# Chained gated MLP: the sums of the weight blocks as GpSimd adds, the chain's copies ahead of GeLU, the first blocks' splits behind the last softmax

## The chip, the cores and the metric

The kernel runs on one core of one Trainium2 chip. The metric is the device time of one execution in microseconds (us). Engines by the names of the profile: PE is TensorE (matmuls), PEld its weight loads, DVE is VectorE, ACT is ScalarE, POOL is GpSimd, SP issues most of the transfers. POOL can also issue transfers; a transfer issued there may add to what lies at its destination ("adding transfer" below).

## The reference, cut to what matters

Two layers; each has a token mixer, a cross-attention and a gated MLP. The change touches the gated MLP and the end of the attention ahead of it.

```python
def conv_ffn(x, norm, w_up, dw_w, dw_b, w_down):
    h = rms_norm(x, norm) @ w_up
    g = causal_dwconv(h[..., :D_FF], dw_w, dw_b)
    u = h[..., D_FF:]
    return (jax.nn.gelu(g) * u) @ w_down

def trunk(x, mem, ...):
    for layer in range(DEPTH):
        ...
        x = x + cross_attn(x, mem, ...)
        x = x + conv_ffn(x, f_norm[layer], f_w_up[layer], f_dw_w[layer], f_dw_b[layer], f_w_down[layer])
    ...
```

The sequence has 512 positions, D_MODEL is 1024, the hidden width D_FF is 3072, and everything is float32.

## The kernel before, in words

**Precision.** A float32 operand is split into a high part (a copy to fp32r by ACT, "high") and a low part (what is left, a subtraction by DVE, "low"). A product is three matmuls: high by high (L186), high by low (L187, L188).

**A unit of the MLP.** The hidden width is cut into 24 chunks of 128 columns per layer, and a unit c computes one chunk of the gate and of the up branch. Two of the 24 are computed plainly ahead (the opening); units 2 to 23 use a scheme of seven products in place of eight, in which sums of blocks of the weights meet sums of blocks of the activations. The blocks of the weights of a chunk are a11, a12, a22 and four sums, s1 to s4. A unit's products, in PE's order, are s1, s2, a12, s3, then (units with c of 4 and more) 24 matmuls of the down projection, then a11 of the next unit, s4, a22. They are chained through PSUM: a product's bank is copied on by ACT (L946, L960, L927), and the next product that accumulates in that bank waits for the copy.

**The sums of the weights.** Class Blocks holds the tiles of one chunk. `load` fetches one 512 KB tile `raw`, whose first half is `r` and whose second is `z`; `load_second` fetches a12 and a22 (tiles `wa`, 256 KB each). The sums are formed in place: once a block has been split by `high` (L814) and `low` (L821), `low` issues the next sum. After a11, z is added to r (L824). After s3, a22 is added to z and to r (L827, two adds). After s2, a12 is added to r (L829). Each of the four is an adding transfer that POOL issues, 256 KB from SBUF to SBUF. There are 22 chunks in each of two layers, so 176 of them; the attention (whose blocks are made with `ring`) uses the same class for 6 pairs, 24 transfers more.

**What sets the order.** Inside a unit the engines run what the code issues in that order: ACT, DVE and POOL are in order, and a waiting instruction holds up what stands behind it. `gating` is a generator that carries the elementwise work of unit c (gate convolution L894 and L897, GeLU L899, product L913, splits L916 and L918) into unit c+1; each `next(left)` in `unit` issues one step of it. The down projection's two banks are first loaded with X by ACT (`down.bank`, L854) and are copied home later (L859).

**The end of the attention.** `prepare` splits blocks of the first MLP chunk inside the attention. `scores(3)`, `transpose(3)`, `back(...)` are the last head's scores, its transposes and the output projections; `score.last` is the last instruction of the softmax so far issued, and `tc.issue_after` keeps what it encloses behind that instruction in program order.

Of the kernel before, what the change touches and what calls it, by code (L numbers as in the profile page):

```python
# [13 lines left out]
ALU = mybir.AluOpType  # L14
# [47 lines left out]
def trunk(ctx: ExitStack, tc: tile.TileContext, I: dict, out: list):  # L62
    nc = tc.nc
    V, A, G, PE = nc.vector, nc.scalar, nc.gpsimd, nc.tensor
# [30 lines left out]
    def tmp_f(n=T):  # L95
        return tmp.tile([P, n], F32, tag="tmp", name=nm("tmp"))

    def main_ps():
        return psum.tile([P, T], F32, tag="mm", name=nm("mm"))
# [70 lines left out]
    def add(out, a, b):  # L170
        V.tensor_tensor(out, a, b, op=ALU.add)  # L171
        return out
# [6 lines left out]
    def low(src, hi, lo=None):  # L179
        lo = act_r() if lo is None else lo  # L180
        V.tensor_tensor(lo, src, hi.bitcast(F32), op=ALU.subtract)  # L181
        return hi, lo
# [54 lines left out]
    class Scaled:  # L237
# [39 lines left out]
        def low(self, c):  # L277
            self.x[c] = low(*self.x[c])
# [191 lines left out]
    def attention(layer, norm, mem, nxt, six, up):  # L470
# [51 lines left out]
        def scores(h):  # L522
            for half in range(2):
                for _ in score(h, half):
                    pass
# [8 lines left out]
        def turned(h):  # L534
            hs = [high(pt) for pt in ps[h]]
            ps[h] = [low(*x) for x in zip(ps[h], hs)]
# [9 lines left out]
        def mixed(h):  # L546
            for d, out in enumerate(mix(h)):
                o[2 * h + d] = split(out)
# [40 lines left out]
        def unit(i, before):  # L589
# [59 lines left out]
            if i == 2:  # L649
                end(3, "a11")  # L650
            q[2 * h] = low(g, hi)
            p = m("a22", six.T4)
            transpose(i)
# [45 lines left out]
        def prepare(*names):  # L699
            for name in names:  # L700
                up.high(name)
                up.low(name)

        back(0, range(4))
        mixed(2)
        prepare("a11", "a22")
        scores(3)
        back(0, range(4, 6))
        back(4, range(6))
# [69 lines left out]
    class Blocks:  # L779
# [39 lines left out]
        def low(self, name):  # L819
            hi, lo = self.w[name]  # L820
            V.tensor_tensor(lo, self.block(name), hi.bitcast(F32), op=ALU.subtract)  # L821

            if name == "a11":
                G.dma_start(self.r, self.z, accum_op=ALU.add)  # L824
            elif name == "s3":
                for block in (self.r, self.z) if self.ring else (self.z, self.r):
                    G.dma_start(block, self.a22, accum_op=ALU.add)  # L827
            elif name == "s2":
                G.dma_start(self.r, self.a12, accum_op=ALU.add)  # L829

    def pairs_of(layer):
        return {c: Blocks(I["wpair"][layer * (CF - PLAIN) + c - PLAIN]) for c in range(PLAIN, CF)}
# [1 line left out]
    def ffn(layer, norm, nxt, seven, pairs):  # L834
# [37 lines left out]
        def high(c, name):  # L872
            if c in pairs and (c, name) not in done:
                pairs[c].high(name)

        def low(c, name):
            if c in pairs and (c, name) not in done:
                pairs[c].low(name)
                done.add((c, name))

        def both(c, name):
            high(c, name)
            low(c, name)

        def times_r(out, ps, at):
            V.tensor_tensor(out[:, at], ps, norm.r[:, at], op=ALU.mult)
# [15 lines left out]
        def gating(c, g, f, u, F, H):  # L902
            add(g[:, right_half], H, u[:, :M])
            V.tensor_tensor(g[:, right_half], g[:, right_half], norm.r[:, right_half], op=ALU.mult)
            conv = gate_conv(c, g)
            y = next(conv)
            yield
            times_r(f, F, left_half)
            next(conv)
            yield  # L910
            next(conv)
            yield
            V.scalar_tensor_tensor(y, f, -1.0, y, op0=ALU.mult, op1=ALU.mult)  # L913
            yield
            ys[c] = act_r(), act_r()
            A.activation(ys[c][0], y, AF.Copy)  # L916
            yield
            V.tensor_tensor(ys[c][1], y, ys[c][0].bitcast(F32), op=ALU.subtract)  # L918

        def m(c, ps, block, j, first=True):  # L920
            seven.product(ps, pairs[c].w[block], j, first)

        def ahead(c):

            G, F = main_ps()[:, :M], main_ps()[:, :M]
            m(c, G, "a11", seven.B11)
            A.activation(F, G, AF.Copy)  # L927
            return G, F

        def unit(c):  # L930

            nonlocal left, chains
            G, F = chains
            down, seeded = downs.get(c), c > GC
            H = main_ps()[:, :M]
            m(c, H, "s1", seven.T1)
            high(c + 1, "s3")
            next(left, None)
            low(c + 1, "s3")
            if c == first:  # L940
                both(c + 2, "a11")

            m(c, F, "s2", seven.T2, False)
            next(left, None)
            u, f, g = tmp_f(), tmp_f(), tmp_f()
            A.activation(u[:, :M], F, AF.Copy)  # L946
            next(left, None)
            high(c + 1, "a22")

            m(c, G, "a12", seven.B21, False)  # L950
            next(left, None)
            if down:
                d = [down.bank(i, seeded) for i in range(2)]
            next(left, None)
            low(c + 1, "a22")
            times_r(g, G, left_half)
            high(c, "s4")

            m(c, F, "s3", seven.T3, False)
            A.activation(u[:, M:], F, AF.Copy)  # L960
            low(c, "s4")
            add(f[:, right_half], H, u[:, M:])
            V.tensor_tensor(f[:, right_half], f[:, right_half], norm.r[:, right_half], op=ALU.mult)
            both(c + 2, "a11")
            high(c + 1, "a12")
            low(c + 1, "a12")
            if down:
                for ks in (range(GC - 1), (GC - 1,)):
                    for i in range(2):
                        down.products(i, d[i], seeded, ks)  # L970
            if c + 3 in pairs:
                pairs[c + 3].load()
            if c + 2 in pairs and c > first:
                pairs[c + 2].load_second()
            if c >= GC - 1 and c + 1 in downs:
                downs[c + 1].w.high()
                downs[c + 1].w.low()
            if c + 2 in downs and c + 2 <= CF:
                downs[c + 2].load()
            high(c + 1, "s1")  # L980
            low(c + 1, "s1")
            high(c + 1, "s2")
            low(c + 1, "s2")
            if down:
                down.home(0, d[0], seeded)

            if c + 1 in pairs:
                chains = ahead(c + 1)
            if down:
                down.home(1, d[1], seeded)  # L990

            m(c, H, "s4", seven.B22, False)
            m(c, F, "a22", seven.T4, False)
            left = gating(c, g, f, u, F, H)
            next(left)
# [81 lines left out]
        left, chains = None, None  # L1077
# [7 lines left out]
        with tc.manual_schedule(engines=ORDERED):  # L1085
            opening()
            for c in range(PLAIN, CF):
                unit(c)
            for _ in left:
                pass  # L1090
# [711 lines left out]
    six = mixer(n0, n1)  # L1802
    pairs = pairs_of(0)
    mem, parked = ffn(0, n2, n3, attention(0, n1, mem, n2, six, pairs[PLAIN]), pairs)
    six = conformer(n3, n4, mem, parked)
    pairs = pairs_of(1)
    ffn(1, n5, None, attention(1, n4, mem, n5, six, pairs[PLAIN]), pairs)


# [76 lines left out]
```

## Time and profile before

| what | us |
|---|---|
| median of 3 runs | 1436.37 (1435.02 to 1438.07) |
| the profiled execution's own time | 1440.97 |
| its span in the trace | 1439.2 |
| layer 0: attention, MLP | about 255 to 346, 346 to 740 |
| layer 1: attention, MLP | about 935 to 1036, 1040 to 1395 |

A row of the timeline reads: start, length (both us), engine, line of the kernel, operation, output and input tiles, their shape, and in brackets the idle time of the engine ahead of it with what ended it. Rows of one engine can overlap by some hundredths, since an instruction's fill and drain are counted. A row of the windows reads: the stretch and its length, then busy us and instructions of PE, PEld, DVE, ACT and POOL, then the granted clock of TensorE (1.00 is full), the busy share of the DMA engines, and GB/s.

### The profile page before, as it was taken

How to read it: one execution, taken by the hardware profiler on the slowest of the kernel's cores; microseconds unless marked ns; L12 is line 12 of the kernel's file. 1: busy time of each engine (PE TensorE's matmuls, PEld its weight loads, DVE VectorE, ACT ScalarE, POOL GpSimd, SP SyncE). 2: the span in 40 equal slices, each digit the busy share in tenths (PEclk: the TensorE clock that was granted, in tenths of full speed). 3: DMA queues.
4: the chain of work that ended last, by engine and by line, in shares of the span. 5: the costliest groups of instructions: out<-in, count | busy, mean ns of one | idle time of the engine just before them, and what ended most of it. 6: DMA issues, size and time to landing. Idle time of an engine off the chain costs nothing.

```text
span 1439.2 us, 22840 instructions
## 1 busy us (share of the span) xinstructions
PE 1421.0 (99%) x8650; PEld 1263.3 (88%) x8650; DVE 1079.1 (75%) x1796; ACT 910.2 (63%) x1592; POOL 317.4 (22%) x333
## 2 busy tenths in 40 slices
PE   9999999999999999999999999999998999999998
PEld 8888888988999999999888777899888999999997
DVE  6987776778876666666789997877787666676665
ACT  7668755667556666666655557667654666666664
POOL 0012310100122222222009991011002222222211
PEclk9999999999999999999999999999999999999999
DMA  8522242544487777777432364345438777777751
GB/s 302 194 88 89 88 132 69 118 108 146 115 197 170 173 175 166 170 176 155 133 117 88 118 183 143 92 96 132 116 104 183 175 174 170 164 177 166 164 123 59
DMA packets 80318, 205.36 MB, mean 143 GB/s; under 512 B 9040, under 2 KB 9552, under 8 KB 80208
## 3 DMA queue, kind: packets, MB, share of 16 engines
q1 hardware_dynamic: 51120, 151.20, 34.0%
q0 software_dynamic: 28800, 52.44, 21.4%
q8 instruction: 67, 1.10, 0.3%
q14 instruction: 43, 0.35, 0.1%
q10 hardware_dynamic: 288, 0.27, 0.1%
HBM read 146.21 MB, written 2.10 MB: 103 GB/s over the span
## 4 chain that ended last, share of the span: by engine, by line
PE 82%; issue 6%; DMA 4%; DVE 3%; POOL 2%; ACT 2%; SPq 0%; POOLq 0%; DVEq 0%; ACTq 0%
PE mm L187 19%; PE mm L186 19%; PE mm L188 19%; PE aux L186 7%; PE aux L187 7%; PE aux L188 7%; PE mm L458 2%; DMA raw<-wa 1%; DMA raw<-raw 1%; DMA raw<-in_wv 1%; DMA wa<-in_wpair 1%; DVE wlo L167 1%; POOL actf L1487 1%; POOL act L167 1%; PE aux L532 1%
## 5 line engine op out<-in xcount | busy, mean ns | idle before, releaser
L186 PE MATMUL mm<-act,whi 128*128 128x512 f32 (+2 forms) x1061 | 369.2, 349 | 1.1 <-ACT whi L803 1.1
L187 PE MATMUL mm<-act,whi 128*128 128x512 f32 (+2 forms) x1061 | 369.3, 348 | 0.8 <-DVE act L181 0.4
L188 PE MATMUL mm<-act,wlo 128*128 128x512 f32 (+2 forms) x1061 | 369.0, 348 | 0.0
L186 PEld LDWEIGHTS mm<-act,whi 128*128 128x128 f32 x1061 | 200.5, 189 | 29.2 <-ACT whi L803 1.5
L187 PEld LDWEIGHTS mm<-act,whi 128*128 128x128 f32 x1061 | 200.7, 189 | 28.2 <-DVE act L167 1.0
L188 PEld LDWEIGHTS mm<-act,wlo 128*128 128x128 f32 x1061 | 200.7, 189 | 24.9 <-DVE wlo L167 0.6
L186 PE MATMUL mm<-bigr,bigr 128*128 128x256 f32 x704 | 199.8, 284 | 5.0 <-ACT tmp L946 5.0
L188 PE MATMUL mm<-bigr,bigr 128*128 128x256 f32 x704 | 199.8, 284 | 0.1
L187 PE MATMUL mm<-bigr,bigr 128*128 128x256 f32 x704 | 199.6, 284 | 0.0
L186 PE MATMUL aux<-act,whi 128*128 128x512 f32 x399 | 156.2, 391 | 0.0
L187 PE MATMUL aux<-act,whi 128*128 128x512 f32 x399 | 156.0, 391 | 0.0
L188 PE MATMUL aux<-act,wlo 128*128 128x512 f32 x399 | 155.5, 390 | 0.0
L827 POOL DMA_DIRECT2D raw<-wa x100 | 88.4, 904 | 283.9 <-DVE bigr L821 151.1
L166 ACT ACTIVATE whi<-raw 128x1024 fp32r<-128x1024 f32 (+1 forms) x95 | 96.7, 1022 | 85.9 <-PE mm L187 46.3
L814 ACT ACTIVATE bigr<-raw 128x512 fp32r<-128x512 f32 x176 | 109.5, 624 | 55.1 <-DVE wlo L203 38.5
L186 PEld LDWEIGHTS mm<-bigr,bigr 128*128 128x128 f32 x704 | 135.4, 192 | 5.6 <-ACT tmp L946 5.6
L171 DVE TENSOR_TENSOR tmp<-mm,tmp 128x256 f32<-128x256 f32 x130 | 54.0, 420 | 110.1 <-PE mm L188 109.6
L188 PEld LDWEIGHTS mm<-bigr,bigr 128*128 128x128 f32 x704 | 135.5, 193 | 0.5 <-DVE bigr L821 0.5
L187 PEld LDWEIGHTS mm<-bigr,bigr 128*128 128x128 f32 x704 | 135.4, 192 | 0.0
L821 DVE TENSOR_TENSOR bigr<-raw,bigr 128x512 fp32r<-128x512 f32 x176 | 121.0, 688 | 12.9 <-ACT bigr L814 9.5
L824 POOL DMA_DIRECT2D raw<-raw x50 | 43.3, 867 | 390.5 <-DVE wlo L821 229.8
L167 DVE TENSOR_TENSOR wlo<-raw,whi 128x1024 fp32r<-128x1024 f32 (+1 forms) x75 | 90.4, 1211 | 20.8 <-ACT whi L166 20.3
(353 smaller groups left out, 3067.5 us busy)
## 6 DMA issues: line engine op xcount, KB each, us to landing
raw<-wa POOLq DMA_DIRECT2D x150, 256.0 KB, 4.0
wa<-in_wpair SPq DMA_DIRECT2D x88, 256.0 KB, 3.8
raw<-in_wpair SPq DMA_DIRECT2D x44, 512.0 KB, 3.9
big<-in_wdown SPq DMA_DIRECT2D x44, 512.0 KB, 4.0
raw<-raw POOLq DMA_DIRECT2D x50, 256.0 KB, 5.0
raw<-in_pw SPq DMA_DIRECT2D x24, 512.0 KB, 3.3
raw<-in_win SPq DMA_DIRECT2D x20, 512.0 KB, 3.3
raw<-in_wk SPq DMA_DIRECT2D x16, 512.0 KB, 3.5
```

The source lines that it names most:

```text
L166: A.activation(hi, src, AF.Copy)
L167: fetched[1] = (eng or V).tensor_tensor(lo, src, hi.bitcast(F32), op=ALU.subtract)
L171: V.tensor_tensor(out, a, b, op=ALU.add)
L186: PE.matmul(ps, wh, xh, start=first, stop=False, skip_group_check=onto)
L187: PE.matmul(ps, wh, xl, start=False, stop=False, skip_group_check=onto)
L188: PE.matmul(ps, wl, xh, start=False, stop=last, skip_group_check=onto)
L458: PE.matmul(p, m[j], x, start=k == 0 and j == 0 and x is hi, stop=k == C - 1 and x is lo)
L532: PE.transpose(pt[:, qc * P : (qc + 1) * P], es[h][qc // 2][:, j : j + P], ident)
L814: A.activation(self.w[name][0], self.block(name), AF.Copy)
L821: V.tensor_tensor(lo, self.block(name), hi.bitcast(F32), op=ALU.subtract)
L824: G.dma_start(self.r, self.z, accum_op=ALU.add)
L827: G.dma_start(block, self.a22, accum_op=ALU.add)
```

## The change

1. The 176 adds of the MLP's blocks become TENSOR_TENSOR instructions on GpSimd, 128 partitions by 512 elements each, read from and written to SBUF. Those of the attention (`ring`) stay adding transfers.
2. In a unit, the copy of F to u (L946 before, L952 in the changed code) and the loading of the down projection's two banks (L854, L861) are issued ahead of GeLU (L899, L906).
3. The splits of a11 and a22 of each layer's first MLP chunk are enclosed in `tc.issue_after(score.last)`, so that they stand behind the softmax of head 2.

```diff
         back(0, range(4))
         mixed(2)
-        prepare("a11", "a22")
+        with tc.issue_after(score.last):
+            prepare("a11", "a22")
         scores(3)
...
             if name == "a11":
-                G.dma_start(self.r, self.z, accum_op=ALU.add)
+                self.plus(self.r, self.z)
             elif name == "s3":
                 for block in (self.r, self.z) if self.ring else (self.z, self.r):
-                    G.dma_start(block, self.a22, accum_op=ALU.add)
+                    self.plus(block, self.a22)
             elif name == "s2":
-                G.dma_start(self.r, self.a12, accum_op=ALU.add)
+                self.plus(self.r, self.a12)
+
+        def plus(self, block, other):
+            if self.ring:
+                G.dma_start(block, other, accum_op=ALU.add)
+            else:
+                G.tensor_tensor(block, block, other, op=ALU.add)
...
             m(c, F, "s2", seven.T2, False)
-            next(left, None)
             u, f, g = tmp_f(), tmp_f(), tmp_f()
             A.activation(u[:, :M], F, AF.Copy)
+            if down:
+                d = [down.bank(i, seeded) for i in range(2)]
+            next(left, None)
             next(left, None)
             high(c + 1, "a22")

             m(c, G, "a12", seven.B21, False)
             next(left, None)
-            if down:
-                d = [down.bank(i, seeded) for i in range(2)]
             next(left, None)
             low(c + 1, "a22")
```

On ACT, in a unit in the middle of layer 0's MLP, before: the gate convolution's first step (L894), the high part of s3 (L814), GeLU (L899), the u copy (L946), a22's high part, the high part of the gated product (L916), the two banks (L854), s4's high part, the second u copy (L960).

```order
L894 ACTIVATE tmp_5268<-tmp_5130,par 128x512
L814 ACTIVATE bigr_5283<-raw_5030 128x512
L899 ACTIVATE tmp_5268<-tmp_5268 128x512
L946 ACTIVATE tmp_5304<-mm_5227 128x256
L814 ACTIVATE bigr_5309<-wa_5208 128x512
L916 ACTIVATE act_5323<-tmp_5268 128x512
L854 ACTIVATE aux_5326<-x 128x512
L854 ACTIVATE aux_5328<-x 128x512
L814 ACTIVATE bigr_5333<-raw_4854 128x512
L960 ACTIVATE tmp_5304<-mm_5227 128x256
```

The same place of the changed kernel, whose lines are numbered higher (L815 is L814 before, L906 is L899, L952 is L946, L861 is L854, L923 is L916):

```order
L901 ACTIVATE tmp_5268<-tmp_5129,par 128x512
L815 ACTIVATE bigr_5283<-raw_5030 128x512
L952 ACTIVATE tmp_5303<-mm_5227 128x256
L861 ACTIVATE aux_5307<-x 128x512
L861 ACTIVATE aux_5309<-x 128x512
L906 ACTIVATE tmp_5268<-tmp_5268 128x512
L815 ACTIVATE bigr_5313<-wa_5208 128x512
L923 ACTIVATE act_5327<-tmp_5268 128x512
L815 ACTIVATE bigr_5333<-raw_4854 128x512
L967 ACTIVATE tmp_5303<-mm_5227 128x256
```

The copy and the two banks stand ahead of GeLU now, and what follows GeLU follows it later by two bank loads; the second u copy keeps its place.

On POOL, in the same layer, before (one row is one block's step; x2 are the two adds of a22):

```order
L827 DMA raw_5910<-wa_6088 128x512 x2
L824 DMA raw_6086<-raw_6086 128x512
L829 DMA raw_5910<-wa_6090 128x512
L827 DMA raw_6086<-wa_6264 128x512 x2
L824 DMA raw_6262<-raw_6262 128x512
```

And in the changed kernel:

```order
L836 TENSOR_TENSOR raw_5910<-raw_5910,wa_6088 128x512 x2
L836 TENSOR_TENSOR raw_6086<-raw_6086 128x512
L836 TENSOR_TENSOR raw_5910<-raw_5910,wa_6090 128x512
L836 TENSOR_TENSOR raw_6086<-raw_6086,wa_6264 128x512 x2
L836 TENSOR_TENSOR raw_6262<-raw_6262 128x512
```

The order on POOL is the same; each issue of a transfer has become the add itself.

On ACT, at the end of layer 0's attention, before: the split of a22 (wa_3042) stands ahead of the exponentials of head 1 (L510).

```order
L803 ACTIVATE wlo_2651<-raw_2327 128x512
L814 ACTIVATE bigr_3086<-wa_3042 128x512
L510 ACTIVATE tmp_2670,sm_2674<-tmp_2670,mx_2669,rq_2251 128x256 x2
L803 ACTIVATE whi_2691<-raw_2325 128x512
L803 ACTIVATE wlo_2693<-wa_2331 128x512
```

In the changed kernel it stands 29 rows further on, behind the softmax of head 2 and the copies of its transposes (L176), ahead of L658:

```order
L176 ACTIVATE act_2997<-tmp_2804 128x512
L815 ACTIVATE whi_3081<-raw_3040 128x512
L176 ACTIVATE act_3026<-aux_3015 128x512
L176 ACTIVATE act_3028<-aux_3016 128x512
L815 ACTIVATE bigr_3086<-wa_3042 128x512
L658 ACTIVATE act_3034<-tmp_2803 128x512
```

The a11 split (whi_3081) stands where it stood. On DVE the low part of a22 moves in the same way, behind head 2's last two splits (L181); in layer 1 both move alike.

## Prediction

> **What bounds the kernel now.** I read the page's head, then a window in the middle of an MLP, PE's waits, and the timeline around the longest of them.
>
> ```profile
> span 1439.2 us, 22840 instructions
> PE 1421.0 (99%) x8650; PEld 1263.3 (88%) x8650; DVE 1079.1 (75%) x1796; ACT 910.2 (63%) x1592; POOL 317.4 (22%) x333
> ...
> 520.00:580.00 60.00, 60.00 (x424) 56.56 (x423) 40.39 (x69) 37.37 (x70) 13.46 (x16) 1.00 0.75 169
> ```
>
> TensorE is busy for 1421.0 of 1439.2 us, and for all of the 60 us in mid-MLP, at the full granted clock (1.00). There DVE is busy 40.39, ACT 37.37 and POOL 13.46 us. The change removes no matmul, so it can win only what PE waits, and what the clock loses behind a wait. PE's waits that touch the change, in all, in times and the longest:
>
> ```profile
> PE mm L186 <- ACT tmp L946: 5.0, 3, 3.7
> PE mm L186 <- ACT whi L803: 1.1, 2, 0.7
> PE mm L188 <- DVE whi L821: 0.4, 2, 0.2
> PE mm L186 <- DVE tmp L171: 0.4, 1, 0.4
> ```
>
> The two longest waits for the u copy (L946) are both for product s3 of unit 4, one in each layer:
>
> ```profile
> 406.45 0.39 PE L186 MATMUL mm<-bigr,bigr 128*128 128x256 f32 x1 [1.16 <-ACT tmp L946]
> ...
> 1089.84 0.86 POOL L824 DMA_DIRECT2D raw<-raw  x1 [4.31 <-DMA wa<-in_wpair]
> ...
> 1098.46 0.63 ACT L814 ACTIVATE bigr<-raw 128x512 fp32r<-128x512 f32 x1 [4.33 <-DMA raw<-raw]
> 1099.00 0.61 ACT L899 ACTIVATE tmp<-tmp 128x512 f32<-128x512 f32 x1
> 1099.52 0.36 ACT L946 ACTIVATE tmp<-mm 128x256 f32<-128x256 f32 x1
> ...
> 1099.93 0.39 PE L186 MATMUL mm<-bigr,bigr 128*128 128x256 f32 x1 [3.67 <-ACT tmp L946]
> ```
>
> In layer 1 POOL issues an adding transfer at 1089.84, and ACT stands until it has landed, at 1098.4, 8.6 us later. Only then come the split (1098.46), GeLU (1099.00) and the copy (1099.52), for which PE has waited 3.67 us. In layer 0 the same place costs 1.16. After the long wait the clock falls:
>
> ```profile
> 1100.00:1102.00 2.00, 2.00 (x12) 2.00 (x12) 1.30 (x3) 1.55 (x3) 0.86 (x1) 0.63 0.90 93
> 1102.00:1104.00 2.00, 2.00 (x7) 1.61 (x7) 1.97 (x5) 1.55 (x4) 0.00 (x0) 0.52 0.97 210
> ...
> 406.50:410.00 3.50, 3.50 (x21) 3.17 (x22) 2.80 (x6) 2.56 (x6) 0.66 (x1) 1.00 0.81 153
> ```
>
> At 0.63 and 0.52 the two stretches of 2 us lose 0.74 + 0.96 = 1.70 us of matmul time. After layer 0's wait of 1.16 the clock stays 1.00: only the long wait pays that.
>
> **The change, part by part.**
>
> *The splits behind the softmax.* Each attention has one place where ACT waits for the load of a22 ahead of softmax work:
>
> ```profile
> 279.57 0.63 ACT L814 ACTIVATE bigr<-wa 128x512 fp32r<-128x512 f32 x1 [3.80 <-DMA wa<-in_wpair]
> ...
> 281.95 0.38 PE L186 MATMUL mm<-act,whi 128*128 128x256 f32 x1 [0.66 <-ACT whi L803]
> ```
>
> PE's wait of 0.66 us goes, as do its twin in layer 1 (1.1 for the two, by the table of waits) and the two behind them for the low part (0.4): 1.5 us. But the split is now issued ahead of the last head's softmax:
>
> ```profile
> 312.34 0.68 DVE L501 TENSOR_TENSOR tmp<-aux,rs 128x512 f32<-128x512 f32 x1
> ...
> 316.61 0.91 ACT L518 ACTIVATE tmp<-tmp,sm 128x256 f32<-128x256 f32 x2 [0.23 <-DVE sm L515]
> ...
> 317.07 1.26 PE L532 MATMUL aux<-ident,tmp 128*128 128x128 f32 x8
> ```
>
> The chain from DVE's scaling of the scores (312.34) to ACT's weights (316.61) ends just as PE starts the transposes that read them. The split's low part stands ahead of it on DVE with some 0.6 us, so the transposes start that much later. Between nothing and 0.6 in both layers I take 1.0 in all given back: **-0.5**, bounds -1.5 and -0.3; with a second wait behind it, +0.5.
>
> *The adds on GpSimd.* Two prices count: the time of an add, and what it does to DVE. No add of these operands on POOL stands in this MLP; the nearest rows are the mixer's, of the same shape, and the conformer's.
>
> ```profile
> 118.62 1.22 DVE L1284 TENSOR_TENSOR_SCAN big<-big,big 128x512 f32<-128x512 f32 x1
> 119.77 2.25 DVE L1284 TENSOR_TENSOR_SCAN big<-big,big 128x512 f32<-128x512 f32 x1
> 119.32 1.62 POOL L1293 TENSOR_TENSOR tmp<-tmp,big 128x512 f32<-128x512 f32 x1 [12.93 <-ACT tmp L1290]
> 120.90 2.21 POOL L1293 TENSOR_TENSOR tmp<-tmp,big 128x512 f32<-128x512 f32 x1
> ...
> L1487 POOL TENSOR_TENSOR actf<-actf,tmp x39: 1237/1287/1319, 761.9 to 848.7; 128x510 f32<-128x510 f32 x5, 128x509 f32<-128x509 f32 x5, 128x508 f32<-128x508 f32 x5, 128x507 f32<-128x507 f32 x5
> L1496 DVE SCALAR_TENSOR_TENSOR aux<-h,par,aux x120: 717/732/749, 758.0 to 864.2; 128x505 f32<-128x505 f32 x5, 128x504 f32<-128x504 f32 x5, 128x503 f32<-128x503 f32 x5, 128x502 f32<-128x502 f32 x5
> ```
>
> The first scan runs 1.22 us and ends at 119.84. POOL's add, begun at 119.32, ends at 120.94, 1.10 us after that; the second scan takes 2.25 instead of 1.22 and ends at 122.02; the second add ends at 123.11, 1.09 later. So the two take turns: an instruction of DVE with two inputs in SBUF and an add of GpSimd don't overlap, and an add holds DVE for up to 1.1 us. The conformer's taps on DVE (L1496, one large input in SBUF, the other in PSUM) run at 717 to 749 ns beside 39 adds of POOL: they aren't held.
>
> The SBUF — State Buffer page of the Trainium skill, section "Who interferes with whom", has the same line between the two: only an instruction with two SBUF inputs meets a GpSimd instruction that reads SBUF, and whoever issues first keeps the other out to its end. The rows agree; were all of DVE's instructions held instead, the delay below would come near its upper bound.
>
> In steady units that fits. A unit recurs after 15.54 us:
>
> ```profile
> 556.39 0.42 DVE L171 TENSOR_TENSOR tmp<-mm,tmp 128x256 f32<-128x256 f32 x1 [2.98 <-PE mm L188]
> 571.93 0.42 DVE L171 TENSOR_TENSOR tmp<-mm,tmp 128x256 f32<-128x256 f32 x1 [2.98 <-PE mm L188]
> 560.71 0.39 ACT L946 ACTIVATE tmp<-mm 128x256 f32<-128x256 f32 x1 [0.28 <-PE mm L188]
> ```
>
> DVE's share of it is 40.39 x 15.54 / 60 = 10.46 us, and four adds add at most 4 x 1.1 = 4.4: 14.9, under 15.54, and DVE has 2.98 us idle in one piece before each next unit. The moved copy (0.39) and banks cost nothing here either: ACT waited for PE before the copy (0.28), so it starts no earlier; GeLU now follows two bank loads, and DVE's product with it, but the matmuls that need that product are the last quarter of the down projection. I count **0** for some 38 steady units. Without that cover each 0.1 us would cost 3.8.
>
> In the openings it doesn't fit. Units 2 and 3 have no down projection, so a unit is only 7 x 12 matmuls of 0.12 = 10.1 us, and DVE is nearly full. Layer 0, from unit 2's last sum to unit 4's first:
>
> ```profile
> 388.10 1.29 DVE L821 TENSOR_TENSOR bigr<-raw,bigr 128x512 fp32r<-128x512 f32 x2
> ...
> 389.76 0.43 DVE L904 TENSOR_TENSOR tmp<-tmp,r 128x256 f32<-128x256 f32 x1
> ...
> 391.07 1.54 DVE L897 SCALAR_TENSOR_TENSOR tmp<-tmp,par,tmp 128x511 f32<-128x511 f32 x2
> 392.52 0.69 DVE L821 TENSOR_TENSOR bigr<-raw,bigr 128x512 fp32r<-128x512 f32 x1
> 393.37 0.69 DVE L913 SCALAR_TENSOR_TENSOR tmp<-tmp,tmp 128x512 f32<-128x512 f32 x1 [0.16 <-ACT tmp L899]
> ...
> 397.08 0.42 DVE L171 TENSOR_TENSOR tmp<-mm,tmp 128x256 f32<-128x256 f32 x1
> ...
> 399.08 1.22 DVE L203 TENSOR_TENSOR wlo<-big,whi 128x1024 fp32r<-128x1024 f32 x1
> 400.22 0.69 DVE L821 TENSOR_TENSOR bigr<-raw,bigr 128x512 fp32r<-128x512 f32 x1
> ```
>
> I lay the adds between these rows by hand. The a12 add starts at 389.4, when s2's low part is done, and holds L904 to about 390.6. The first a22 add follows at about 391.0 and holds L897 for 1.0. The second follows the split of 392.52 and holds L913 for up to 1.0. Of these 2.8 us DVE's short idle pieces take up 0.9: L171 (397.08) is 1.9 late. The next block's first add then holds L203 for 1.1: the split of 400.22, for which unit 4 starts, is 3.0 late. Between it and 2.2, if one add falls into an idle piece, I take **2.7 us**; the ends are 0 (every add meets instructions with an operand in PSUM) and 5.5 (five adds held in full).
>
> What goes in exchange are the late copies: an add ready some 1.2 us after its start in place of a landing 4 to 8.6 us after its issue, so the split of s2 no longer waits, and the u copy no longer stands behind GeLU. In layer 0, s3 without its wait would start at 406.45 - 1.16 = 405.29; 2.7 later is 407.99: **+1.5**. In layer 1, 1099.93 - 3.67 + 2.7 = 1098.96: **-1.0**, and the clock keeps its 1.7: **-1.7**. The new delays come in pieces too short to lower the clock, as layer 0's 1.16 was.
>
> The sum is -0.5 + 1.5 - 1.0 - 1.7 = **-1.7 us**. The profiled execution took 1440.97 (its span and 1.8 around it) and would take 1439.3; it lies 4.6 above the median of the runs, 1436.37, which I shift by the same: **1434.7**.
>
> **The rivals.**
>
> *B, the adds cost DVE little.* If POOL's adds mostly fall beside L171 and L886, which read PSUM, or into idle pieces, the openings start on time and all waits go: -1.16 - 3.67 - 1.7 - 0.4 (the L171 wait) - 1.5 = -8.4, 1428.0; with half of the delay, 2 x 1.35 back, 1430.7. For it: DVE idles in pieces of 0.2 to 0.9 there. Against: an add starts just when DVE's low part ends, and DVE's next instruction is most often of the kind that is held. It decides at a delay under 1.3. Its time: 1430.
>
> *C, slower: DVE becomes the bound of the steady unit.* The place is every unit from 5 on. It decides where an add holds DVE for more than (15.54 - 10.46) / 4 = 1.27 us. The mixer's 1.1 is below, the conformer's median of 1.287 just above: 4 x 1.287 + 10.46 = 15.61, 38 units x 0.07 = +2.7. A hold of 1.4, between that and the 1.62 that an add shows with its wait, gives 16.06, +0.52 x 38 = +20. I price it halfway, +11: 1446. Against it: a hold counts only while a DVE instruction of the right kind waits. The GPSIMD Engine Reference of the Trainium skill, section "Engine selection", speaks against the change: two-input elementwise work belongs on VectorE, since GpSimd is about twice as slow. By that an add would take, as an estimate from DVE's 0.69, 1.38 us, and the unit 15.98: +17, 1452. The mixer's 1.1 is against it, the conformer's 1.287 nearer to it.
>
> *D, the change doesn't do what it says.* If the split of s2 waits for the load of its `wa` and not for the add (POOL's row of 1089.84 had itself waited 4.31 us for a load), the layer 1 wait stays, and the delay is paid only where it is longer: between -0.5 and +1.5, 1437.
>
> **How the numbers follow.** My forecast (A) has 0.42, B 0.25, C 0.20, D 0.13. A alone spans 1432.5 to 1437.5 (the delay of 1.8 to 3.6 counts in both layers, plus the attention). Below 1428.5 lies a fifth of B, above 1445 half of C: the range is **1428.5 to 1445**. About 0.2%, 2.9 us, is what a measurement of this kernel tells from no change: faster is below 1433.5, slower above 1439.2. Faster holds nearly all of B and a quarter of A, 0.34; slower nearly all of C and a little of A and D, 0.23; the rest, 0.43, is the same.
>
> **What would show it.** Right: POOL's adds of 1.1 to 1.7 us in the place of L824, L827 and L829; in units 2 and 3 some DVE rows with two SBUF inputs 0.4 to 1.1 longer than 0.69; unit 4 starting 2 to 3.5 us later after unit 2 than before; s3 of unit 4 without a wait for the u copy; no granted clock under 0.9 near 1100; no wait for L803 in the attention, and a small new one at the last transposes. In mid-MLP PE busy for 60.00 of 60 us as before. Wrong by B: no longer DVE rows in the openings, and more than 6 us won. Wrong by C: PE waits for DVE (L821, L171) in every unit, and a unit longer than 15.54. Wrong by D: the s2 split in unit 4 of layer 1 still ends a wait of several us, now for `wa`.

## The result and the profile after

The changed kernel takes **1443.22 us** (median of 6 runs, 1442.33 to 1444.92) against 1436.44 (6 runs, 1435.02 to 1440.26) before: ratio **1.0044** (95% interval 1.0031 to 1.0057), 6.8 us slower by the medians, 6.3 by the ratio. Its profiled execution took 1442.87. That lies inside the range on record, but the kernel has become slower where the forecast, 1434.7, was a little faster.

The page's head and a window in mid-MLP of the changed kernel (columns as before: busy us of PE, PEld, DVE, ACT, POOL, clock, DMA share, GB/s):

```profile
span 1441.1 us, 22719 instructions
PE 1423.8 (99%) x8650; PEld 1267.1 (88%) x8650; DVE 1171.2 (81%) x1796; ACT 900.6 (62%) x1592; POOL 422.2 (29%) x333
...
520.00:580.00 60.00, 60.00 (x424) 56.51 (x423) 48.98 (x71) 36.87 (x69) 22.82 (x16) 1.00 0.34 104
```

DVE has 92 us more than before (1171.2 against 1079.1) with the same 1796 instructions, so its instructions have become longer. In mid-MLP PE is still busy for all of the 60 us: DVE went from 40.39 to 48.98, and nothing of it reached PE. PE's waits of the changed kernel:

```profile
PE mm L186 <- DVE tmp L171: 4.9, 4, 1.9
PE mm L186 <- ACT act L274: 1.5, 1, 1.5
...
PE mm L186 <- ACT tmp L952: 1.0, 3, 0.4
```

The waits for L946 (5.0 in all) and L803 are gone or small; 4.9 us for DVE's L171 and 1.5 for ACT's L274 have come. Where they are, in the timeline of layer 0's opening:

```profile
386.13 0.39 PE L186 MATMUL mm<-act,bigr 128*128 128x256 f32 x1 [0.57 <-DVE tmp L171]
...
388.71 1.29 DVE L911 TENSOR_TENSOR tmp<-tmp,r 128x256 f32<-128x256 f32 x1
393.25 1.78 DVE L920 SCALAR_TENSOR_TENSOR tmp<-tmp,tmp 128x512 f32<-128x512 f32 x1 [0.16 <-ACT tmp L906]
399.87 2.29 DVE L203 TENSOR_TENSOR wlo<-big,whi 128x1024 fp32r<-128x1024 f32 x1
...
388.42 2.74 POOL L836 TENSOR_TENSOR raw<-raw,wa 128x512 f32<-128x512 f32 x2 [3.23 <-DVE bigr L822]
393.18 1.30 POOL L836 TENSOR_TENSOR raw<-raw,wa 128x512 f32<-128x512 f32 x1 [2.02 <-DVE bigr L822]
399.43 1.66 POOL L836 TENSOR_TENSOR raw<-raw 128x512 f32<-128x512 f32 x1 [4.95 <-DVE wlo L822]
...
398.35 0.39 PE L186 MATMUL mm<-act,bigr 128*128 128x256 f32 x1 [1.87 <-DVE tmp L171]
```

Each long row of DVE lies beside an add of POOL: the add of 393.18 ends at 394.48, and L920, issued at 393.25, takes 1.78 instead of 0.69; L203 takes 2.29 instead of 1.22; L911 (128x256) 1.29 instead of 0.43. That makes them 1.09, 1.07 and 0.86 longer. PE waits 0.57 for s4 of unit 2 and 1.87 for s4 of unit 3. Behind the second wait the clock falls, and in layer 1 it does so too:

```profile
398.00:400.00 2.00, 1.65 (x9) 1.66 (x10) 1.97 (x5) 0.99 (x2) 0.57 (x1) 0.68 0.67 170
400.00:402.00 2.00, 2.00 (x11) 2.00 (x11) 2.00 (x1) 0.90 (x2) 1.09 (x1) 0.50 0.55 223
...
1095.00:1097.00 2.00, 2.00 (x12) 2.00 (x12) 2.00 (x2) 0.90 (x2) 1.27 (x1) 0.51 0.68 267
1097.00:1099.00 2.00, 2.00 (x12) 1.93 (x12) 1.97 (x5) 0.00 (x0) 0.36 (x1) 0.63 0.00 0
```

That takes about 1.7 us of matmul time each time (2 x 0.49 + 2 x 0.37 in layer 1); what it costs in the end is taken up below. The other place is the seam between layer 0's MLP and layer 1:

```profile
740.72 1.05 PE L314 MATMUL stat<-onesf,tmp 128*128 128x1 f32 x8 [0.32 <-DVE tmp L248]
744.69 0.50 PE L350 MATMUL aux<-act,unit 128*128 128x512 f32 x1 [0.29 <-DVE act L327]
746.70 0.64 PE L186 MATMUL mm<-act,whi 128*128 128x512 f32 x1 [1.50 <-ACT act L274]
...
748.00:750.00 2.00, 2.00 (x7) 1.60 (x6) 2.00 (x5) 1.29 (x3) 0.00 (x0) 0.50 0.03 8
```

Before, the same stretch had one wait of 0.43 and a clock of 1.00:

```profile
743.33 0.50 PE L187 MATMUL mm<-act,whi 128*128 128x512 f32 x1 [0.43 <-DVE act L181]
...
744.00:746.00 2.00, 2.00 (x16) 1.86 (x15) 2.00 (x4) 1.35 (x3) 0.00 (x0) 1.00 0.04 8
```

### The profile page after: what moved, and what is told of

It is laid out like the page before. It is cut to its first block, busy times and chain, and to the rows that moved or that the text cites. A ratio compares the mean times of both kernels' runs of the same rounds, so it can differ in the third digit from the quotient of the medians.

```text
span 1441.1 us, 22719 instructions
## 1 busy us (share of the span) xinstructions
PE 1423.8 (99%) x8650; PEld 1267.1 (88%) x8650; DVE 1171.2 (81%) x1796; ACT 900.6 (62%) x1592; POOL 422.2 (29%) x333
## 4 chain that ended last, share of the span: by engine, by line
PE 82%; DVE 10%; ACT 3%; POOL 2%; issue 2%; DMA 2%; SPq 0%; DVEq 0%; ACTq 0%; POOLq 0%
PE mm L186 19%; PE mm L187 19%; PE mm L188 19%; PE aux L186 7%; PE aux L187 7%; PE aux L188 7%; PE mm L458 2%; DVE wlo L203 1%; DVE bigr L822 1%; DVE wlo L167 1%; DMA raw<-in_wv 1%; DVE tmp L904 1%; POOL actf L1494 1%; ACT whi L166 1%; DVE wlo L822 1%
## 5 line engine op out<-in xcount | busy, mean ns | idle before, releaser
L836 POOL TENSOR_TENSOR raw<-raw,wa 128x512 f32<-128x512 f32 x132 | 183.6, 1404 | 283.2 <-DVE bigr L822 235.7
L815 ACT ACTIVATE bigr<-raw 128x512 fp32r<-128x512 f32 x176 | 108.8, 620 | 125.7 <-DVE wlo L203 122.4
L836 POOL TENSOR_TENSOR raw<-raw 128x512 f32<-128x512 f32 x44 | 73.7, 1675 | 273.5 <-DVE wlo L822 273.5
L904 DVE SCALAR_TENSOR_TENSOR tmp<-tmp,par,tmp 128x511 f32<-128x511 f32 x96 | 75.0, 781 | 24.2 <-ACT tmp L901 22.6
```

Of the source, the lines that this page charges most:

```text
L815: A.activation(self.w[name][0], self.block(name), AF.Copy)
L836: G.tensor_tensor(block, block, other, op=ALU.add)
L904: V.scalar_tensor_tensor(y[:, s:], g[:, : T - s], dw(2 - s), y[:, s:], op0=ALU.mult, op1=ALU.add)
```

## The experiments

Ratios are to runs of the kernel before on the same chip, with 95% intervals; 0.001 is 1.4 us. A ratio is not the quotient of the two medians; where the two tell a different story, both are given. All kernels have the change's code unless the diff says otherwise.

**The kernel before, profiled a second time.** No edit.

> The kernel before, for a second look at its trace: its first profiled execution took 1440.97 us, 4.6 above the median of its runs. Theory A: the wait of 3.67 us ahead of s3 of unit 4 in layer 1 and the clock of 0.63 and 0.52 behind it (1.70 us) belong to that execution and not to the kernel: here the wait is under 1.5 us, the clock stays above 0.9 and the span is near 1435. Theory B: the wait belongs to the kernel; it is there again (3 to 4 us), and the 4.6 us lie elsewhere.

Measured: 1435.59 us for the profiled execution, span 1433.5.

```profile
1088.87 0.86 POOL L824 DMA_DIRECT2D raw<-raw  x1 [4.31 <-DMA wa<-in_wpair]
...
1094.12 0.63 ACT L814 ACTIVATE bigr<-raw 128x512 fp32r<-128x512 f32 x1 [0.96 <-DMA raw<-raw]
...
1095.78 0.39 PE L186 MATMUL mm<-bigr,bigr 128*128 128x256 f32 x1 [0.47 <-ACT tmp L946]
...
1095.00:1097.00 2.00, 1.53 (x13) 1.32 (x12) 1.29 (x3) 1.84 (x4) 1.05 (x2) 1.00 1.09 193
```

The same adding transfer, issued at 1088.87, lets ACT go at 1094.12, 5.3 us later and not 8.6; PE waits 0.47 and not 3.67, and the clock stays 1.00. Theory A: the long wait and its 1.7 us belong to the execution that I had read, not to each one. Layer 0's wait was 0.47 as well. Of the 27 runs of before on that chip, eight took over 1439 us; whether by the same wait, no trace shows.

**The splits behind the softmax alone.**

```diff
-        prepare("a11", "a22")
+        with tc.issue_after(score.last):
+            prepare("a11", "a22")
```

> Only the splits of a11 and a22 behind the last softmax. Theory A: in the trace of the full change, layer 0's attention ended 2.1 us earlier and layer 1's gained 1.5, so this part alone is worth -3.6 (ratio 0.9965 to 0.9985), and PE has no wait for L803 in either attention. Theory B: those gains came from the missing adding transfers, and this part alone gives 0 to -1 (ratio above 0.9992).

Measured: 1434.37 us, ratio 0.9976 (0.9964 to 0.9988), -3.4 us; the medians (1434.37 and 1436.01) lie only 1.6 apart. No wait for L803 is left. Theory A.

**The copies ahead of GeLU alone.** The second part of the change, nothing else.

> Only the u copy and the two banks ahead of GeLU. Theory A: the order on PE at the seam between layer 0's MLP and layer 1 comes with this part, and with it the waits of 0.3, 0.3 and 1.5 us and the clock of 0.86 and 0.71 near 747: +2 to +3.5 (ratio 1.0014 to 1.0025), nothing in the units. Theory B: the seam comes of the adds' times, and this part gives 0 to -1.5, by the u copy's waits ahead of s3 of unit 4.

Measured: 1442.11 us, ratio 1.0037 (1.0019 to 1.0055), +5.3, more than either theory gave. The profiled execution, 1439.47, was the fastest of the ten.

```profile
399.04 0.39 PE L186 MATMUL mm<-act,bigr 128*128 128x256 f32 x1 [0.66 <-DVE tmp L171]
...
745.39 0.49 PE L186 MATMUL mm<-act,whi 128*128 128x512 f32 x1 [1.50 <-ACT act L274]
...
747.00:749.00 2.00, 2.00 (x8) 1.72 (x7) 2.00 (x4) 1.35 (x3) 0.00 (x0) 0.50 0.04 8
```

The seam's wait and low clock come with this part, with no add on GpSimd in the kernel. Beside it s4 of unit 3 waits 0.66 in each layer: there GeLU (394.38) now stands behind the u copy, for which ACT waits 1.93 for PE (L945, 394.10), and the chain to L171 ends later.

**The adds on GpSimd alone.** The first part of the change, nothing else.

> Only the adds on GpSimd. Theory A: the openings are DVE-bound, an add holds DVE for 1.1 us, s4 of unit 3 waits about 1.9 us in each layer and the clock falls near 0.6 behind it: +5 to +8 (ratio 1.0035 to 1.0055) against a usual execution of before. Theory B: what the adds cost in the openings they give back at s3 of unit 4: -1.5 to +1.5. Both: units of 15.54 us in mid-MLP.

Measured: 1481.19 us, ratio **1.0301** (1.0282 to 1.0320), +43 us. Neither theory; and a unit of mid-MLP takes 16.49 (561.94 to 578.43, the starts of the same matmul), not 15.54.

```profile
PE aux L186 <- ACT aux L860: 24.9, 36, 1.0
...
574.79 0.63 ACT L905 ACTIVATE tmp<-tmp 128x512 f32<-128x512 f32 x1 [1.14 <-DVE tmp L903]
575.37 1.30 POOL L835 TENSOR_TENSOR raw<-raw,wa 128x512 f32<-128x512 f32 x1 [3.38 <-DVE bigr L821]
575.45 1.77 DVE L919 SCALAR_TENSOR_TENSOR tmp<-tmp,tmp 128x512 f32<-128x512 f32 x1 [0.16 <-ACT tmp L905]
577.25 0.63 ACT L922 ACTIVATE act<-tmp 128x512 fp32r<-128x512 f32 x1 [1.04 <-DVE tmp L919]
577.79 1.10 ACT L860 ACTIVATE aux<-x 128x512 f32<-128x512 f32 x2
578.43 0.50 PE L186 MATMUL aux<-act,whi 128*128 128x512 f32 x1 [0.67 <-ACT aux L860]
```

Read upward: PE (578.43) waits for the first bank, which ACT loads at 577.79, behind the split of 577.25, which waits for DVE's product of 575.45, which is held by the add of 575.37. That repeats in 36 units. In the full change the banks stand ahead of GeLU, and there the product starts 0.12 after the add of 562.52 has ended and runs its short time:

```profile
562.25 1.11 ACT L861 ACTIVATE aux<-x 128x512 f32<-128x512 f32 x2
562.52 1.30 POOL L836 TENSOR_TENSOR raw<-raw,wa 128x512 f32<-128x512 f32 x1 [2.02 <-DVE bigr L822]
563.94 0.69 DVE L920 SCALAR_TENSOR_TENSOR tmp<-tmp,tmp 128x512 f32<-128x512 f32 x1 [1.50 <-ACT tmp L906]
```

**The adds with the banks ahead.** Of the second part only the banks are moved; the u copy stays behind GeLU, and the splits stay where they were.

```diff
             m(c, F, "s2", seven.T2, False)
-            next(left, None)
             u, f, g = tmp_f(), tmp_f(), tmp_f()
+            if down:
+                d = [down.bank(i, seeded) for i in range(2)]
+            next(left, None)
             A.activation(u[:, :M], F, AF.Copy)
...
             next(left, None)
-            if down:
-                d = [down.bank(i, seeded) for i in range(2)]
             next(left, None)
```

> The adds on GpSimd, and of the copies ahead of GeLU only the two banks of the down projection; the u copy stays behind GeLU, the splits stay where they were. The adds alone gave 1.0301, with 36 waits of 0.7 to 1.0 us for the banks. Theory A: an add holds the DVE product behind GeLU, the banks stood behind that product's split on ACT, and PE waited for the banks: with the banks ahead those 36 waits are gone and a unit is back at 15.54, ratio 1.004 to 1.010. Rival: the adds make DVE the bound of a unit (units of 16.5 us whatever ACT's order), ratio above 1.025.

Measured: 1447.71 us, ratio 1.0076 (1.0063 to 1.0089), from 1.0301. The 36 waits are gone, and units are back at full PE while DVE stays as loaded:

```profile
520.00:580.00 60.00, 60.00 (x417) 56.17 (x416) 51.40 (x70) 36.48 (x69) 22.68 (x16) 1.00 0.34 104
```

So the banks' place on ACT, and not DVE's sum of work, is what the adds run into in the steady units.

**The full change without the adds.** The first part of the change undone.

> The full change less the adds, which stay adding transfers. Theory A: the copies alone cost at the seam what the first trace shows there (+2.5 to +6), the splits alone give -2 to -3.4, so the two together stand at 0 to +3 (ratio 1.000 to 1.002), and the adds of the full change cost the remaining 4 to 7. Rival: the adds cost nothing once the banks are ahead, and this kernel is as slow as the full change (ratio 1.0044).

Measured: 1437.94 us, ratio 1.0008 (0.9997 to 1.0020). As theory A has it, the adds cost the full change the rest, 0.0036 or 5.2 us. The profiled execution, 1433.69, was the fastest of the twelve; the seam's wait of 1.50 is in it, but the clock stays at 1.00 behind it.

**Adds only in the later chunks, and only in the first.** One line differs from the full change: `if self.ring or self.chunk < 6` here, and `if self.ring or self.chunk >= 6` in the second; each chunk is given its number.

> The full change, but the sums of the chunks 2 to 5 stay adding transfers, so that no GpSimd add falls into units 2 to 4; 18 chunks of each layer keep the adds. Theory A: the adds cost only in the openings; this is within 0.1% of the kernel without adds sent beside it, s4 of unit 3 waits under 0.8 us. Rival: the adds cost in every unit, and this stays within 0.1% of the full change (ratio 1.0044).

> The counterpart of the kernel with late adds: the full change, but only the chunks 2 to 5 of each layer are summed by GpSimd, 16 adds in a layer's opening; the other 18 chunks keep adding transfers. Theory A: the opening carries the cost of the adds: s4 of unit 3 waits 1.9 us with the clock near 0.6 behind it in each layer, ratio 1.0030 to 1.0045. Rival: the cost is spread over the units, ratio 1.0010 to 1.0020.

Measured: late adds alone 1439.57 us, ratio 1.0017 (1.0005 to 1.0029); first chunks alone 1443.08 us, ratio 1.0045 (1.0033 to 1.0057). PE at s4 of unit 3, layer 0, late adds and then first chunks:

```profile
396.85 0.39 PE L186 MATMUL mm<-act,bigr 128*128 128x256 f32 x1 [0.66 <-DVE tmp L171]
...
398.74 0.39 PE L186 MATMUL mm<-act,bigr 128*128 128x256 f32 x1 [1.90 <-DVE tmp L171]
```

32 adds in the two openings cost all that the 176 do; the 144 others cost 0.0009 over the kernel without adds, which the intervals don't tell from nothing. With late adds the openings keep their adding transfers, and in that trace s3 of unit 4 of layer 1 waits 1.86 for the u copy (1096.69). The opening's own price is in the step from 0.66 to 1.90, the 0.55 at s4 of unit 2, and what follows: in layer 0 a wait of 1.13 for s1 of unit 4 at a clock of 1.00, in layer 1 the low clock (0.50) in that wait's place. Theory A had the low clock in both layers.

**The old order in the last unit only.** The full change, with `early` false for the last unit of a layer:

```diff
+            early = c < CF - 1
+            if not early:
+                next(left, None)
             u, f, g = tmp_f(), tmp_f(), tmp_f()
             A.activation(u[:, :M], F, AF.Copy)
-            if down:
-                d = [down.bank(i, seeded) for i in range(2)]
-            next(left, None)
+            if early:
+                if down:
+                    d = [down.bank(i, seeded) for i in range(2)]
+                next(left, None)
             next(left, None)
...
             next(left, None)
+            if down and not early:
+                d = [down.bank(i, seeded) for i in range(2)]
             next(left, None)
```

> The full change, but the last unit of each layer keeps the old order of copies and GeLU, which gives PE back its order of before at the seam. Theory A: the waits of 0.3, 0.3 and 1.5 us near 745 and the low clock behind them go, -2.5 to -4 against the full change (ratio 1.0015 to 1.0030). Rival: the seam's loss is made up by what follows in layer 1, and the ratio stays at 1.004 to 1.005.

Measured: 1440.39 us, ratio 1.0024 (1.0015 to 1.0033), against the full change's 1.0044 (1.0031 to 1.0057, from other runs): some 2.9 us, 0.6 to 5.2 by the two intervals. PE's instructions stand in the order of before again, and of the three waits at the seam one of 0.43 is left, at the place where before had it:

```profile
744.16 0.50 PE L187 MATMUL mm<-act,whi 128*128 128x512 f32 x1 [0.43 <-DVE act L181]
```

**The adds on DVE.** The full change with `V.tensor_tensor` for `G.tensor_tensor` in `plus`.

> The full change with the 176 adds on DVE instead of GpSimd. Theory A (an add on GpSimd keeps DVE out for 1.1 us): an add on DVE takes some 0.6, so the openings are late by less, ratio 1.0020 to 1.0035, and DVE's instructions are all back at their short times (L203 at 1.22, L920 at 0.69). Rival: GpSimd's adds do relieve DVE, and with them on DVE the openings and the units are later than in the full change, ratio above 1.0044.

Measured: 1441.56 us, ratio 1.0040 (1.0025 to 1.0055): not told from the full change, above what theory A gave.

```profile
395.56 0.69 DVE L920 SCALAR_TENSOR_TENSOR tmp<-tmp,tmp 128x512 f32<-128x512 f32 x1
399.56 0.39 PE L186 MATMUL mm<-act,bigr 128*128 128x256 f32 x1 [1.54 <-DVE tmp L171]
400.61 0.69 DVE L836 TENSOR_TENSOR raw<-raw 128x512 f32<-128x512 f32 x1
401.82 1.22 DVE L203 TENSOR_TENSOR wlo<-big,whi 128x1024 fp32r<-128x1024 f32 x1
```

All of DVE's instructions are back at their short times, so the length came of GpSimd's adds, as theory A has it. But the wait is 1.54, hardly less than 1.87: an add of 0.69 in DVE's own queue is always paid, a hold of up to 1.1 by GpSimd only where an add meets something. The opening has no room on DVE for either.

**Versions that keep the adding transfers.** The splits behind the softmax, and the copies ahead of GeLU in units 2 to 5 (`early = c < 6`), or in unit 4 alone (`early = c == 4`).

> No GpSimd adds; the splits behind the softmax as in the change, and the copies ahead of GeLU in units 2 to 5 alone. Theory A: the gain of the splits (-2 to -3.4) and the waits ahead of s3 of unit 4 (2 x 0.5 and up to 5 in some executions) come together: -3.5 to -5.5 (ratio 0.9962 to 0.9976) and no wait for the u copy in either opening. Rival: the copies bring a wait at s4 of unit 3 of the same size (0.7 in the kernel with the copies alone), and the ratio is that of the splits alone, 0.9976 to 0.9985.

> No GpSimd adds; the splits behind the softmax, and the copies ahead of GeLU in unit 4 of each layer alone (the unit where s3 waited for the u copy). Theory A: in unit 3 the moved copies delay GeLU and what follows, and s4 of unit 3 waits 0.67 to 0.88 (as with units 2 to 5); with unit 4 alone those waits go: ratio 0.9960 to 0.9972, the fastest so far. Rival: nothing is gained over units 2 to 5 (0.9972) or over the splits alone (0.9976).

Measured: 1432.61 us, ratio 0.9972 (0.9961 to 0.9983), and 1431.90 us, ratio 0.9964 (0.9949 to 0.9978). Both beat both kernels; whether the copies add anything to the splits (0.9976), and which of the two is faster, the intervals don't tell. The waits at s4 of unit 3 are 0.67 and 0.88 with units 2 to 5, and the u copy's wait, which theory A had gone, is 0.44 in layer 0; with unit 4 alone layer 0 has none and layer 1 one of 0.59. In that trace s3 of unit 4 of layer 0 waits 2.10 for the u copy (405.19) even though it stands ahead of GeLU: ahead of both stands the split of the next unit's s3, which waits for the adding transfer that POOL issued at 397.24.

```profile
397.24 0.86 POOL L825 DMA_DIRECT2D raw<-raw  x1 [4.65 <-DMA raw<-wa]
404.66 0.63 ACT L815 ACTIVATE bigr<-raw 128x512 fp32r<-128x512 f32 x1 [3.28 <-DMA raw<-raw]
405.61 0.39 PE L186 MATMUL mm<-bigr,bigr 128*128 128x256 f32 x1 [2.10 <-ACT tmp L949]
```

So this wait comes and goes between executions and kernels with the landing of one transfer; the moved copies don't remove it.

## Why the prediction was wrong, point by point

**Mid-MLP: right.** I had 0 for 38 units, and PE is busy for 60.00 of 60 us. But I named the wrong cover. I put the moved banks at "nothing" for the copies and never asked what the adds would cost without them. The trials show it: 1.0301 without the moved banks, 1.0076 with them. What I wrote as rival C (a slower unit) did come true with the adds alone, by another way: one held instruction, the product behind GeLU, in a chain that ends in PE, while DVE's sum stayed under the unit's time. The second part of the change pays for the first.

**The attention: right sign, too small.** "I take 1.0 in all given back: -0.5". The splits alone gave -3.4 (-1.7 to -5.2). Matched matmul by matmul with the second profile of before, their trace gains 1.49 in layer 0's attention (249.87 to 290.66) and 1.56 in layer 1's; 0.3 is lost again at layer 0's last transposes, and in the full change nothing is. So two terms were off. The 1.0 given back was near nothing. And the waits were priced by their idle time alone: the two of layer 0 (0.39 and 0.23 in the second profile) cost 1.12 by the starts of the matmuls. Matmuls of 0.28 start 0.12 apart in a row, so a wait also takes the overlap of 0.16, and the first matmul behind it is longer by 0.1.

**The openings: the largest error, +7.6 where I had -1.2.** Starts of products, read from PE's timeline (first matmul of each, us), for the second profile of before and for the changed kernel:

| product | layer 0 before, after | lead or lag | layer 1 before, after | lead or lag |
|---|---|---|---|---|
| a11 of unit 3 | 386.49, 383.97 | -2.52 | 1075.76, 1079.14 | +3.38 |
| s4 of unit 2 | 387.93, 386.13 | -1.80 | 1077.20, 1081.32 | +4.12 |
| s4 of unit 3 | 398.00, 398.35 | +0.35 | 1087.57, 1093.52 | +5.95 |
| a12 of unit 4 | 404.10, 405.69 | +1.59 | 1093.70, 1100.94 | +7.24 |
| s3 of unit 4 | 406.17, 407.13 | +0.96 | 1095.78, 1102.38 | +6.60 |
| s3 of unit 5 | 421.81, 423.25 | +1.44 | 1111.42, 1118.44 | +7.02 |

Over the opening that is +3.96 and +3.64. The mechanism is the one that I laid out by hand: I had L171, for which s4 of unit 3 waits, late by 1.9, and the wait is 1.87. That the two agree so well is partly luck: the adds alone give 1.66, and the moved copies alone, which I had at nothing there, 0.66. Four steps beside it failed.

- The exchange. "In layer 1, 1099.93 - 3.67 + 2.7": the 3.67 was that execution's (the split that waited is the next unit's s3, which I called s2's). In the second profile PE waits 0.47 there, and the moved copies give back 0.6 (a12 to s3 of unit 4 in the table), not 3.67 and 1.16. This and the clock behind it take 3.2 + 1.7 from layer 1's gain, and 0.7 from layer 0's. The sign of it was on the table: the profiled execution lay 4.6 above the median of the runs, outside the range of the three shown, and I shifted the difference to the median as if those 4.6 us were spread evenly. By the second profile, 3.2 of wait and 1.7 of clock at this place make up 4.9 of the 5.4 us between the two executions (1440.97 and 1435.59).
- The clock. "The new delays come in pieces too short to lower the clock". The wait of 1.87 lowered it in both layers of the profiled execution, some 1.7 each time. I had one wait that didn't (1.16) and one that did (3.67), and put the border at the upper end. The step was wrong, but little hangs on it here. The kernel with the old order in the last unit has the same code in the openings, and in its layer 0 the clock stays at 1.00 behind the same wait:

```profile
397.96 0.38 PE L186 MATMUL mm<-act,bigr 128*128 128x256 f32 x1 [1.87 <-DVE tmp L171]
402.47 0.39 PE L188 MATMUL mm<-bigr,bigr 128*128 128x256 f32 x1 [1.14 <-DVE bigr L822]
...
400.00:402.00 2.00, 1.34 (x12) 1.13 (x10) 2.00 (x2) 0.65 (x2) 0.73 (x1) 1.00 0.41 166
```

  There PE waits 1.14 for DVE's split for s1 of unit 4 instead, and from a11 of unit 3 to s3 of unit 5 it loses 4.02, as the full change does with the low clock (3.96). The low clock ran in time in which PE would have waited for DVE.
- The size of the delay. From s4 of unit 2 to a12 of unit 4 the table has 3.39 and 3.12, where I had 2.7 for the start of unit 4. And s4 of unit 2 itself waits 0.57 (0.72 and 0.74 in the table), ahead of the place where my layout began.
- Unit 5. The u copy of unit 5 is late by 0.4 in both layers. I stopped at unit 4. That DVE has not yet caught up is argued, not shown: neither the first chunks' adds alone nor the later ones alone have this wait.

In these terms the +7.6 is my -1.2, plus 5.6 for the exchange and its clock, 1.5 for s4 of unit 2, 1.1 for the start of unit 4, 0.9 for unit 5, less 0.3 because s3's wait gave back 0.63 and not 0.47 in each layer.

**The seam: a term that is missing, about +2.9.** The change alters PE's order at the end of layer 0's MLP, where the order isn't written by hand, and I put nothing on it. The last unit's order of copies decides it, as the trial with that unit alone shows. Matched with the second profile of before, the seam loses 2.8 in the kernel without adds, where the clock stays at 1.00, and 4.2 in the full change, where it falls.

The sum by the trials: splits -3.4; copies and the seam together +4.6 (1.0008 - 0.9976); adds +5.2. That these give the 6.3 of the full change is so by construction and no check. What checks them: the splits and the copies measured apart (0.9976 and 1.0037) make 1.0013, beside 1.0008 measured together; and the traces have -3.1 for the attentions, +7.6 for the openings and +4.2 for the seam, 8.7, beside 7.6 between the two spans (1441.1 and 1433.5), with the changed kernel 1.0 ahead before the first attention begins.

Of the rivals, B's claim that the adds cost DVE little fell. So did D's that the split waits for a load: in the changed kernel ACT's split ahead of s3 of unit 4 in layer 1 (L815 at 1100.96) has no wait. D's time was nearer than mine because it left the layer 1 wait unwon, and a usual execution has no such wait to win.

## What to carry to other kernels

If the profiled execution lies outside the range of the other runs, find out which rows make the difference before a gain is built on them: a long wait on a transfer may be that execution's alone, and a second profile settles it. Moving work from transfers to GpSimd put it in turn with DVE instructions that read two tensors from SBUF (1.78 instead of 0.69 here), so ask not only whether DVE's sum has room, but which held instruction has PE at the end of its chain. And where part of the order is not written by hand, look at every place where the change alters it, far from the edit too.

## What the runs showed of the hardware

- An add of GpSimd (128x512, both inputs in SBUF) takes 1.29 to 1.30 us when it begins free, and a DVE instruction with two inputs in SBUF issued behind its start ends 0.9 to 1.1 later (L911 1.29 against 0.43, L203 2.29 against 1.22). With the adds on DVE the same instructions are at 1.22 and 0.69.
- A wait of PE between 1.5 and 2.1 us lowers the clock in some executions and not in others: in the fourteen traces, 6 of the 9 waits from 1.86 to 2.10 were followed by a stretch at 0.50, and 2 of the 14 from 1.50 to 1.70. In the kernel with the splits alone a wait of 2.02 passes; in the one with copies in unit 4 alone a wait of 2.10 doesn't (windows behind each):

```profile
1096.00:1098.00 2.00, 2.00 (x13) 1.74 (x12) 1.84 (x4) 1.94 (x5) 0.02 (x1) 1.00 0.96 158
...
407.00:409.00 2.00, 2.00 (x10) 1.81 (x9) 1.50 (x3) 1.66 (x4) 0.16 (x1) 0.50 1.03 151
```

  The seam's wait of 1.50 lowered it to 0.50 in two kernels (the full change and the copies alone) and left it at 1.00 in four (without adds, with late adds, with the first chunks' adds, and with the adds on DVE). The Trainium skill's page "TensorE: Matmul & The Clock Gate", in "HAM oscillation — how this bites in real kernels", puts the rule at idle gaps of over about 3.4 us; here waits of 1.5 to 2.1 were enough at times. That it is only at times would fit its remark in "What's actually happening" that the window of activity runs free; no trace here shows that window.
- The landing of one adding transfer of 256 KB to SBUF took at most 5.3 us in one execution and 8.6 in another, from its issue to the instruction that waited for it, at the same place of the same program.
